# LayerNorm of all channels in token halves, with the last channel block's first-half convolution inside its own products

## The chip, the cores and the metric

One core of a Trainium2 chip runs the whole program. The metric is device time in microseconds (us) from the start of the program to its end; lower is better. The time given for a kernel is the median of its runs.

## The reference

One encoder layer on 512 tokens of 2048 channels, in float32: an RMSNorm; a pointwise product to 4096 channels, gated (`a * sigmoid(gate)`); a depthwise convolution of width 31 along the tokens; a LayerNorm over the channels of each token with gain and bias; `silu`; a second pointwise product (2048 to 2048), added to the input; then an RMSNorm, a squared-ReLU MLP of 8192 channels, another residual addition and a last RMSNorm. The change touches the end of the convolution, the LayerNorm and the beginning of the second pointwise product:

```python
u = lax.conv_general_dilated(u, w_dw[:, None, :], window_strides=(1,), padding=[(15, 15)], ...) + b_dw
u = jax.nn.silu(layer_norm(u, ln_g, ln_b))
return u @ w_pw2 + b_pw2
```

## The kernel before, in words

Channels lie on the 128 partitions and tokens along the free axis, so 2048 channels are 16 blocks of [128, 512]. Every float32 operand of a large product is split into a high part (ScalarE, ACT) and a low part (VectorE, DVE), and each product is three matmuls (`mm3`, L199): high by high, high by low, low by high. A weight piece is split by `split_hi` (L155, ACT) and `split_lo` (L164, DVE or POOL).

**First product and convolution.** `pw1` (L335) makes the two banks of one channel block j: 16 input blocks by 2 outputs by 3 matmuls. `glu` (L373) gates them into a padded buffer `u`. `conv_parts` (L390) returns the convolution of a block as three shares of the 31 taps: `on_pool` (ACT multiplies, POOL adds), `on_vector` (one multiply-add on DVE for each tap) and, for the last block alone, taps on TensorE (PE) by `conv_pe` (L452), whose stationary operands are 31-tap diagonals `dgw` (built at L520). The convolution of block j-1 runs beside the products of block j.

**The last block** (15) has no later products to run beside. Its products come in two token parts: `banks_a` (tokens 0 to 271, L526) and `banks_b` (L534). All work after them stands in one hand-written block (L619 to L705), inside which DVE, ACT and POOL keep the written order; PE keeps the written order throughout. It takes the first token half: 7 taps on POOL, 17 on DVE, 7 on PE; then the second half: 9, 14 and 8. `ln_sums` and `ln_last` (L543, L548) sum the channels by one-column matmuls into the bank `cols`; `ln_m2` to `ln_power` make variance and its power -1/2; `ln_mean` and `ln_scale` (L559, L584) spread mean and scale over the partitions by a matmul against a diagonal.

**LayerNorm of one block** is a chain of five instructions: `ln_a` (POOL adds the mean), `ln_b` (DVE multiplies by the scale; ACT applies Silu; ACT casts the high part), `ln_c` (DVE subtracts to get the low part). Blocks 0 to 7 are done in token halves, first all of half 0, later half 1; blocks 8 to 15 in full width by `ln` (L608).

**Second product.** `group` (L742) makes four banks from 16 blocks. In the first group (`split=4`) the blocks 0 to 7 (pieces 0 to 3) are multiplied for token half 0, then for half 1, then the blocks 8 to 15 in full width. At the places `LN_AT` in it stand `second_sums`, `second_mean` and `second_scale` (L707 to L736): the statistics of half 1 and the rest of the LayerNorm.

Of the kernel before, what the change touches and what calls it, by code (L numbers as in the profile page):

```python
# [14 lines left out]
P = 128  # L15
# [18 lines left out]
POOL_TAPS = [5, 5, 6, 5] * 3 + [6, 5, 9]  # L34
LAST_POOL, LAST_PE = (7, 9), (7, 8)
PE_TAPS = max(LAST_PE)
# [3 lines left out]
SUM_AT, SCALE_AT = (0, 15), (1, 13)  # L40
PE_AT = (2, 4)
SPLIT_AT = (1, 4)
NEXT_AT = 7
TAIL = (20, 7, 4, 2, 3)
LN_AT = ((0, 2, 2), (0, 3, 0), (0, 3, 1))
UNIT = 256
# [5 lines left out]
def conformer_layer(ctx: ExitStack, tc: tile.TileContext, xT, vecs, wdw, w1, w2, wupb, wdn, outT):  # L52
# [337 lines left out]
    def conv_parts(j, npool, t0=0, n=T, npe=0):  # L390
# [23 lines left out]
        def on_vector(c):  # L414
            acc = chain[(c - npool) % 2]
            src = acc
            if c == npool and j >= SHIFT_FROM:
                src = box["kb"][:, t0 : t0 + n]
# [32 lines left out]

    def conv_pe(acce, t0, n, i0, i1, npe):  # L452

        u = ubuf[(NK - 1) % 3]
        for i in range(i0, i1):
            c = CW - 1 - i
# [3 lines left out]
                rhs=u[:, t0 + c : t0 + c + n],  # L460
                start=i == 0,
                stop=i == npe - 1,
# [70 lines left out]
    sums(last - 1)  # L533
    banks_b = pw1(last, HT, HT)  # L534
    S, Q = box["S"], box["Q"]
# [7 lines left out]
    def ln_sums(h):  # L543
        t0 = HT * h
        colsum(cols, 4 * h, [S, box[last - 1][0]], t0, 2, h == 0, False, 1)
        colsum(cols, 4 * h + 2, [Q, box[last - 1][1]], t0, 2, False, False)

    def ln_last(h):  # L548
        t0 = HT * h
        colsum(cols, 4 * h, [vlast], t0, 2, False, True, 1)  # L550
        colsum(cols, 4 * h + 2, [sqlast], t0, 2, False, True)

# [3 lines left out]
    def ln_diag_mean(h):  # L556
        st[h]["dm"] = diag(cols[:, 4 * h : 4 * h + 2], f"mu{h}", ph1)

    def ln_mean(h):  # L559

        b = rstd[:, 0:HT]
        spread(st[h]["dm"], b, h == 1)
        nc.scalar.copy(out=mus[:, halves[h]], in_=b)

    def ln_m2(h):
        st[h]["m2"] = ph1.tile([P, 2], F32, name=f"m2{h}", bufs=1)
        nc.scalar.activation(out=st[h]["m2"], in_=cols[:, 4 * h : 4 * h + 2], func=AF.Square)

    def ln_var(h):
        st[h]["var"] = ph1.tile([P, 2], F32, name=f"var{h}", bufs=1)  # L570
        nc.vector.tensor_sub(out=st[h]["var"], in0=cols[:, 4 * h + 2 : 4 * h + 4], in1=st[h]["m2"])

# [13 lines left out]


    tmp = {}

    def ln_a(k, h):  # L590
        t = ph1.tile([P, T], F32, tag=("pc", "tg")[k % 2], name=f"lt{k}_{h}", bufs=2 - k % 2)[:, 0:HT]
        nc.gpsimd.tensor_add(out=t, in0=vg[k // 4][:, k % 4, halves[h]], in1=mus[:, halves[h]])
        tmp["t", k, h] = t

    def ln_b(k, h):
        t = ph1.tile([P, T], F32, tag=("vt", "ta")[k % 2], name=f"lu{k}_{h}", bufs=2 - k % 2)[:, 0:HT]
        nc.vector.tensor_mul(out=t, in0=tmp["t", k, h], in1=scale_of[h])
# [9 lines left out]

    def ln(k):  # L608
        t = ph1.tile([P, T], F32, tag="pc", name=f"lt{k}")
        nc.gpsimd.tensor_add(out=t, in0=vg[k // 4][:, k % 4], in1=mus)  # L610
        t2 = ph1.tile([P, T], F32, tag="vt", name=f"lu{k}")
        for h in range(2):
            nc.vector.tensor_mul(out=t2[:, halves[h]], in0=t[:, halves[h]], in1=scale_of[h])
        s = ph1.tile([P, T], F32, tag="pm", name=f"ls{k}", bufs=3)
        nc.scalar.activation(out=s, in_=t2, func=AF.Silu, scale=col(C_LNG, k), bias=col(C_LNB, k))
        nc.scalar.copy(out=sh[k], in_=s)
        nc.vector.tensor_sub(out=sl[k], in0=s, in1=sh[k].bitcast(F32))

    with tc.manual_schedule(engines=ordered):  # L619

        acc0, rstd = bank("mm", "acce0"), bank("x", "acce1")
        npool, npe = LAST_POOL[0], LAST_PE[0]
        on_pool, on_vector, join, vt, pc = conv_parts(last, npool, 0, HT, npe)
        npool1, npe1 = LAST_POOL[1], LAST_PE[1]
        on_pool1, on_vector1, join1, vt1, pc1 = conv_parts(last, npool1, HT, HT, npe1)
# [6 lines left out]

        for c in range(npool):
            on_pool(c)
            if c in SPLIT_AT:
                split_hi(n_p1 + 1 + SPLIT_AT.index(c))
        for c in range(npool, TAIL[0]):
            on_vector(c)
        conv_pe(acc0, 0, HT, 0, npe, npe)
        glu(last, *(b[:, EDGE - HT : HT] for b in banks_b), EDGE)  # L640
        some(1)
        cols = bank("y", "cols")
        scale_of = cols[:, HT:T], rstd[:, HT:T]
        ln_sums(0)
        conv_pe(rstd, HT, HT, 0, PE_AT[0], npe1)
        for c in range(TAIL[0], CW - npe - 2):
            on_vector(c)
        v = vlast[:, halves[0]]
        nc.vector.tensor_add(out=v, in0=pc[-1], in1=acc0[:, halves[0]])
        for c in range(CW - npe - 2, CW - npe):  # L650
            on_vector(c)
        join()
        nc.vector.tensor_add(out=v, in0=v, in1=vt)

        for c in range(5):
            on_pool1(c)
            if c == 2:
                split_hi(n_p1 + 3)
        ln_square(0)
        for c in range(5, TAIL[1]):  # L660
            on_pool1(c)
        some(TAIL[2])
        ln_last(0)
        conv_pe(rstd, HT, HT, PE_AT[0], PE_AT[1], npe1)
        ln_m2(0)
        ln_diag_mean(0)
        ln_var(0)
        ln_guard(0)
        ln_power(0)
        some(3)  # L670
        ln_mean(0)

        nc.scalar.activation(out=tiny, in_=ones[:, 0:1], func=AF.Silu)
        ln_diag_scale(0)
        ln_scale(0)
        conv_pe(rstd, HT, HT, PE_AT[1], npe1, npe1)
        ln_a(0, 0)
        ln_a(1, 0)
        for c in range(TAIL[1], npool1):
            on_pool1(c)  # L680
        some(TAIL[3])
        for k in range(0, 8, 2):
            if k < 6:
                ln_a(k + 2, 0)
                ln_a(k + 3, 0)
            ln_b(k, 0)
            ln_b(k + 1, 0)
            if k == 0:
                ln_sums(1)
            if k == 2:  # L690
                v = vlast[:, halves[1]]
                nc.vector.tensor_add(out=v, in0=pc1[-1], in1=rstd[:, halves[1]])
                some(99)
                ln_c(k, 0)
                join1()
                nc.vector.tensor_add(out=v, in0=v, in1=vt1)
                ln_square(1)
                ln_c(k + 1, 0)
            else:
                some(TAIL[4])  # L700
                ln_c(k, 0)
                ln_c(k + 1, 0)
            if k < 4:
                split_lo(n_p1 + 1 + k // 2, nc.vector)
        split_lo(n_p1 + 3, nc.gpsimd)  # L705

    def second_sums():  # L707
        ln_last(1)
        with tc.manual_schedule(engines=ordered):
# [3 lines left out]
            ln_guard(1)  # L713
            ln_power(1)
            ln_diag_scale(1)

    def second_mean():
        ln_mean(1)

    def second_scale():  # L720
        ln_scale(1)
        with tc.manual_schedule(engines=ordered):
            ln_a(0, 1)
            for k in range(8):
                if k < 7:
                    ln_a(k + 1, 1)
                ln_b(k, 1)
                if k:
                    ln_c(k - 1, 1)
                if k == NEXT_AT:  # L730
                    split_hi(n_p1 + 4)
                    split_lo(n_p1 + 4, nc.gpsimd)
            ln_c(7, 1)
        for k in range(8, NK):
            ln(k)
        p1.close()  # L736
# [72 lines left out]
    for g in range(4):  # L809
# [249 lines left out]
```

## Time and profile before

| | |
|---|---|
| median of 3 runs | 1942.65 us (1941.12 to 1948.48) |
| the profiled execution, its own time | 1946.38 us |
| its span, first to last instruction | 1944.6 us |
| PE busy in the span | 1913.9 us (98%) |
| first half of block 15's last products to the end of the first group of the second product | 347.2 to 436.4 us |

The profile shows one execution. A row of the timeline gives start, duration, engine, line, operation, and in brackets the idle time before it with what ended it; "x14" means 14 records merged. A float32 matmul of a tap, a sum or a spread has two records. [...]

### The profile page before, as it was taken

The page shows a single profiled execution, that of the slowest core. Times are in us where ns is not written, and L with a number is a line of the kernel's source. Part 1 is how long each engine was busy: PE and PEld are TensorE (multiplying, and loading weights), DVE is VectorE, ACT ScalarE, POOL GpSimd, SP SyncE. Part 2 cuts the span into 40 slices and gives each one's busy share as a digit, 9 for nine tenths or more (in the row PEclk, how much of TensorE's full clock was granted, in tenths as well). Part 3 has the DMA queues.
Part 4 walks back from the last instruction along what each step waited for, and adds up shares of the span by engine and source line. Part 5 has one row for each costly group of instructions (what it writes and reads, how often), then busy time and mean ns, then how long its engine had stood idle before and what let it go on. Part 6 is the DMA issues. An engine that isn't in the chain of part 4 may idle for free.

```text
span 1944.6 us, 27603 instructions
## 1 busy us (share of the span) xinstructions
PE 1913.9 (98%) x11192; PEld 1702.6 (88%) x11192; DVE 1389.9 (71%) x1911; ACT 741.1 (38%) x907; POOL 356.7 (18%) x243
## 2 busy tenths in 40 slices
PE   9999999899999999999999999999999999999997
PEld 7888888888879898998989899898989989899987
DVE  6999999875467675766767576676757667576844
ACT  6544444554344232423324233332423324242443
POOL 1789998741120000000000000000000000000000
PEclk9999999999999999999999999999999999999999
DMA  7332333143322333333233232323323233332332
GB/s 245 98 98 87 98 98 110 43 141 96 98 78 79 117 101 91 113 87 110 86 108 109 88 119 79 118 87 103 115 87 109 87 119 93 92 116 89 109 98 99
DMA packets 134558, 199.23 MB, mean 102 GB/s; under 512 B 7200, under 2 KB 72992, under 8 KB 134432
## 3 DMA queue, kind: packets, MB, share of 16 engines
q1 hardware_dynamic: 134288, 197.41, 33.1%
q8 instruction: 87, 1.43, 0.3%
q14 instruction: 39, 0.32, 0.1%
q10 hardware_dynamic: 144, 0.07, 0.0%
HBM read 193.27 MB, written 4.19 MB: 102 GB/s over the span
## 4 chain that ended last, share of the span: by engine, by line
issue 70%; PE 25%; DVE 4%; ACT 1%; POOL 1%; DMA 0%; SPq 0%; POOLq 0%; DVEq 0%; ACTq 0%
PE g L201 3%; PE g L202 3%; PE g L200 3%; PE pa L202 2%; PE pa L201 2%; PE pa L200 2%; PE pg L202 2%; PE pg L201 2%; PE pg L200 2%; DVE acc L426 2%; PE pa L363 1%; PE pg L363 1%; DVE slot L604 0%; POOL Q L841 0%; DMA wr<-w 0%
## 5 line engine op out<-in xcount | busy, mean ns | idle before, releaser
L162 ACT CAST wh<-wr 128x1024 fp32r<-128x1024 f32 x215 | 226.0, 1051 | 451.0 <-PE g L201 315.3
L200 PE MATMUL g<-z,wh 128*128 128x512 f32 (+1 forms) x1016 | 390.6, 384 | 0.0
L201 PE MATMUL g<-z,wh 128*128 128x512 f32 (+1 forms) x1016 | 390.3, 384 | 0.0
L202 PE MATMUL g<-z,wl 128*128 128x512 f32 (+1 forms) x1016 | 390.1, 384 | 0.0
L167 DVE TENSOR_TENSOR wl<-wr,wh 128x1024 fp32r<-128x1024 f32 x157 | 197.1, 1256 | 214.4 <-ACT wh L162 214.2
L202 PE MATMUL u<-slot,wl 128*128 128x256 f32 x1120 | 320.1, 286 | 3.6 <-DVE wl L186 2.6
L200 PE MATMUL u<-slot,wh 128*128 128x256 f32 x1120 | 318.1, 284 | 0.0
L201 PE MATMUL u<-slot,wh 128*128 128x256 f32 x1120 | 317.9, 284 | 0.0
L186 DVE TENSOR_TENSOR wl<-ws,wh 128x1024 fp32r<-128x1024 f32 x128 | 156.9, 1225 | 188.0 <-ACT wh L185 187.0
L248 POOL TENSOR_TENSOR rr_fin<-ms_fin,mhalf 128x2 f32<-128x2 f32 x2 | 1.4, 697 | 1341.5 <-DVE ms_fin L246 1341.5
L185 ACT CAST wh<-ws 128x1024 fp32r<-128x1024 f32 x128 | 134.4, 1050 | 289.9 <-DVE ws L183 135.1
L426 DVE SCALAR_TENSOR_TENSOR acc<-u,wd,acc 128x512 f32<-128x512 f32 (+1 forms) x362 | 239.0, 730 | 3.2 <-ACT acc L422 2.5
L202 PEld LDWEIGHTS g<-z,wl 128*128 128x128 f32 x1016 | 190.9, 188 | 37.8
L200 PEld LDWEIGHTS g<-z,wh 128*128 128x128 f32 x1016 | 191.0, 188 | 37.5
L201 PEld LDWEIGHTS g<-z,wh 128*128 128x128 f32 x1016 | 191.0, 188 | 37.1
L202 PEld LDWEIGHTS u<-slot,wl 128*128 128x128 f32 x1120 | 216.1, 193 | 7.4 <-DVE wl L186 6.6
L200 PEld LDWEIGHTS u<-slot,wh 128*128 128x128 f32 x1120 | 216.2, 193 | 0.0
L201 PEld LDWEIGHTS u<-slot,wh 128*128 128x128 f32 x1120 | 216.1, 193 | 0.0
L202 PE MATMUL u<-T,wl 128*128 128x256 f32 x672 | 190.6, 284 | 1.6 <-DVE wl L186 1.5
L200 PE MATMUL u<-T,wh 128*128 128x256 f32 x672 | 190.7, 284 | 1.0 <-ACT wh L185 1.0
L201 PE MATMUL u<-T,wh 128*128 128x256 f32 x672 | 190.1, 283 | 0.0
L178 ACT CAST wh<-wr 128x768 fp32r<-128x768 f32 x128 | 106.9, 835 | 214.5 <-PE g L201 123.0
(199 smaller groups left out, 3448.8 us busy)
## 6 DMA issues: line engine op xcount, KB each, us to landing
wr<-wupb SPq DMA_DIRECT2D x128, 512.0 KB, 3.6
wr<-wdn SPq DMA_DIRECT2D x128, 512.0 KB, 3.7
wr<-w SPq DMA_DIRECT2D x128, 256.0 KB, 3.2
wr<-w SPq DMA_DIRECT2D x32, 512.0 KB, 3.6
h<-xT SPq DMA_DIRECT2D x4, 1024.0 KB, 11.3
outT<-h SPq DMA_DIRECT2D x14, 256.0 KB, 2.8
x<-xT SPq DMA_DIRECT2D x6, 512.0 KB, 8.1
x<-xT SPq DMA_DIRECT2D x4, 256.0 KB, 4.9
```

Of the source, the lines that this page charges most:

```text
L162: nc.scalar.copy(out=prepped[i][0], in_=r)
L167: eng.tensor_tensor(out=lo, in0=r, in1=hi.bitcast(F32), op=ALU.subtract)
L178: nc.scalar.copy(out=hr, in_=r[:, :, 1:4])
L185: nc.scalar.copy(out=hs, in_=s)
L186: nc.vector.tensor_tensor(out=ls, in0=s, in1=hs.bitcast(F32), op=ALU.subtract)
L200: nc.tensor.matmul(out, lhsT=wh, rhs=xh, start=start, stop=False, **kw)
L201: nc.tensor.matmul(out, lhsT=wh, rhs=xl, start=False, stop=False, **kw)
L202: nc.tensor.matmul(out, lhsT=wl, rhs=xh, start=False, stop=stop, **kw)
L248: nc.gpsimd.tensor_tensor(out=r, in0=ms, in1=mhalf[:, 0:n], op=ALU.pow)
L363: nc.tensor.matmul(banks[j][s], lhsT=w[:, s, k % 2, c], rhs=x, start=k == 0 and x is ah[k] and w is wh, stop=stop)
L426: nc.vector.scalar_tensor_tensor(out=acc if c < end - 1 else vt, in0=u[:, c : c + n], scalar=wd[:, j, c : c + 1], in1=src, op0=ALU.mult, o ...
```

## The change

- The first token half of block 15 takes 7 taps on POOL, 8 on DVE and 16 on PE (before 7, 17 and 7); the second half 9, 12 and 10 (before 9, 14 and 8). `dgw` holds 16 diagonals, not 8.
- The first half's taps stand inside the products of `banks_b` before input block 8, and its sums, variance and power before input block 13 (`LAST_AT`).
- The LayerNorm is done in 32 units of one block and one token half, all 16 blocks of half 0 first, then all 16 of half 1 (`ln_to`). The full-width `ln` is gone.
- The first group splits at 5 pieces: blocks 0 to 9 in token halves, 10 to 15 in full width. The places `LN_AT` move.
- Both `split_lo` that ran on POOL here run on DVE. The shift `kb` has a copy `kbs` in SBUF for the second half.

```diff
-LAST_POOL, LAST_PE = (7, 9), (7, 8)
+LAST_POOL, LAST_PE = (7, 9), (16, 10)
+LAST_AT = (8, 13)
+SPLIT = 5
-LN_AT = ((0, 2, 2), (0, 3, 0), (0, 3, 1))
+LN_AT = ((0, 2, 0), (0, 3, 0), (0, 3, 2))
...
+    units = [(k, h) for h in range(2) for k in range(NK)]
...
     def ln_a(k, h):
-        t = ph1.tile([P, T], F32, tag=("pc", "tg")[k % 2], name=f"lt{k}_{h}", bufs=2 - k % 2)[:, 0:HT]
+        tag = ("tg", "ta", "lt")[(16 * h + k) % 3]
+        t = ph1.tile([P, HT if tag == "lt" else T], F32, tag=tag, name=f"lt{k}_{h}", bufs=1)[:, 0:HT]
...
+    def ln_to(n, ahead):
+
+        while done["c"] < n:
+            while done["a"] < min(done["b"] + 3, ahead):
+                ln_a(*units[done["a"]])
+                done["a"] += 1
+            if done["b"] < n:
+                ln_b(*units[done["b"]])
+                done["b"] += 1
+            if done["c"] < done["b"] - 1 or done["b"] == n:
+                ln_c(*units[done["c"]])
+                done["c"] += 1
...
+    def first_taps():
+        with tc.manual_schedule(engines=ordered):
+            for c in range(npool):
+                on_pool(c)
+                if c in SPLIT_AT:
+                    split_hi(n_p1 + 1 + SPLIT_AT.index(c))
+            for c in range(npool, CW - npe):
+                on_vector(c)
+            conv_pe(acc0, 0, HT, npe, True)
+
+    def first_sums():
+        box["cols"] = bank("y", "cols")
+        with tc.manual_schedule(engines=ordered):
+            join()
...
+            ln_square(0)
+            ln_sums(0)
+            ln_last(0)
+            ln_m2(0)
+            ln_diag_mean(0)
+            ln_var(0)
+            ln_guard(0)
+            ln_power(0)
+            split_lo(n_p1 + 1, nc.vector)
+            ln_diag_scale(0)
+
+    banks_b = pw1(last, HT, HT, hooks=dict(zip(LAST_AT, (first_taps, first_sums))))
...
+        glu(last, *(b[:, EDGE - HT : HT] for b in banks_b), EDGE)
+
+        nc.scalar.activation(out=tiny, in_=ones[:, 0:1], func=AF.Silu)
+        ln_mean(0)
+        ln_scale(0)
...
+        conv_pe(rstd, HT, HT, npe1, False)
+        split_lo(n_p1 + 2, nc.vector)
+        some(3)
+        for c in range(4):
             on_pool1(c)
...
+        split_hi(n_p1 + 3)
+        for n in range(1, 5):
+            ln_to(n, NK)
+            for c in range(4 + 2 * (n - 1), min(4 + 2 * n, npool1)):
+                on_pool1(c)
+            some(3)
+        ln_to(6, NK)
+        v = vlast[:, halves[1]]
+        nc.vector.tensor_add(out=v, in0=pc1[-1], in1=rstd[:, halves[1]])
+        some(99)
+        join1()
+        nc.vector.tensor_add(out=v, in0=v, in1=vt1)
+        ln_square(1)
+        ln_sums(1)
+        ln_to(8, NK)
+        split_lo(n_p1 + 3, nc.vector)
 
     def second_sums():
         ln_last(1)
...
             ln_power(1)
+            split_hi(n_p1 + 4)
+            ln_to(10, NK)
             ln_diag_scale(1)
+            split_lo(n_p1 + 4, nc.vector)
+            ln_to(12, NK)
 
     def second_mean():
-        ln_mean(1)
+        with tc.manual_schedule(engines=ordered):
+            ln_mean(1)
+            ln_to(14, NK + 1)
 
     def second_scale():
         ln_scale(1)
         with tc.manual_schedule(engines=ordered):
...
+            ln_to(2 * NK, 2 * NK)
         p1.close()
...
-        banks = group(NK, sh, sl, hooks, split=4 if g == 0 else 0)
+        banks = group(NK, sh, sl, hooks, split=SPLIT if g == 0 else 0)
```

## Rows read from the trace of the kernel before

**Rows 1.** The page's part 1: busy us (share of the span) xinstructions by engine.

```profile
PE 1913.9 (98%) x11192; PEld 1702.6 (88%) x11192; DVE 1389.9 (71%) x1911; ACT 741.1 (38%) x907; POOL 356.7 (18%) x243
```

**Rows 2.** Windows: length; busy us of PE, PEld, DVE, ACT, POOL; granted clock; DMA; GB/s.

```profile
347.20:358.70 11.50, 11.50 (x98) 11.50 (x97) 11.33 (x22) 7.40 (x12) 9.55 (x9) 1.00 0.01 2
358.70:375.80 17.10, 15.47 (x76) 12.96 (x74) 14.66 (x39) 10.69 (x23) 12.28 (x18) 0.80 0.00 0
375.80:436.40 60.60, 53.70 (x303) 47.58 (x303) 44.56 (x72) 31.98 (x56) 28.36 (x24) 0.92 0.41 137
...
386.20:393.60 7.40, 7.34 (x34) 7.23 (x35) 2.76 (x10) 1.98 (x5) 0.71 (x1) 0.54 0.25 71
...
412.90:417.00 4.10, 4.08 (x12) 3.22 (x13) 4.10 (x7) 1.43 (x2) 3.33 (x2) 0.62 0.57 167
```

**Rows 3.** PE's waits, 340 to 440 us: total us, times, longest us.

```profile
PE g L201 <- DVE slot L604: 3.7, 5, 2.3
PE g L201 <- DVE slot L617: 3.0, 1, 3.0
```

**Rows 4.** PE's timeline, from the last products' end to the first group's end.

```profile
358.73 3.18 PE L457 MATMUL acce<-u,dgw 128*128 128x256 f32 x14
363.54 0.58 PE L234 MATMUL cols<-invd,S 128*128 128x1 f32 x4 [1.63 <-DVE acc L426]
...
365.31 1.27 PE L457 MATMUL acce<-u,dgw 128*128 128x256 f32 x4
...
417.84 0.39 PE L200 MATMUL g<-slot,wh 128*128 128x512 f32 x1
...
434.16 0.39 PE L200 MATMUL g<-slot,wh 128*128 128x512 f32 x1
```

**Rows 5.** ACT's timeline: the diagonals early in the program, then the LayerNorm.

```profile
27.17 2.45 ACT L520 ACTIVATE dgw<-ident,wd 128x128 f32<-128x128 f32 x8
...
370.92 0.37 ACT L563 COPY mus<-acce 128x256 f32<-128x256 f32 x1 [2.60 <-PE acce L223]
371.31 1.28 ACT L673 ACT_TABLE_LOAD   x1
...
372.71 0.89 ACT L409 ACTIVATE pm<-u,wd 128x256 f32<-128x256 f32 x2
...
382.50 0.60 ACT L599 ACTIVATE ls<-lu,vec 128x256 f32<-128x256 f32 x1 [1.39 <-DVE lu L597]
383.13 0.41 ACT L600 CAST slot<-ls 128x256 fp32r<-128x256 f32 x1
```

**Rows 6.** DVE's timeline: taps, gate, LayerNorm, a weight split, the first group's output.

```profile
357.13 4.40 DVE L426 SCALAR_TENSOR_TENSOR acc<-u,wd,acc 128x256 f32<-128x256 f32 x11
...
362.39 0.47 DVE L381 SCALAR_TENSOR_TENSOR u<-ta,vec,tg 128x240 f32<-128x240 f32 x1 [0.25 <-ACT tg L378]
...
382.05 0.74 DVE L597 TENSOR_TENSOR lu<-lt,cols 128x256 f32<-128x256 f32 x2
...
390.43 0.42 DVE L213 TENSOR_TENSOR dg_mu<-ident,cols 128x256 f32<-128x256 f32 x1 [2.03 <-ACT m L567]
...
390.83 0.42 DVE L604 TENSOR_TENSOR slot<-ls,slot 128x256 fp32r<-128x256 f32 x1
...
394.96 0.42 DVE L597 TENSOR_TENSOR lu<-lt,acce 128x256 f32<-128x256 f32 x1 [2.38 <-POOL lt L592]
...
401.87 0.41 DVE L597 TENSOR_TENSOR lu<-lt,acce 128x256 f32<-128x256 f32 x1
...
413.45 1.21 DVE L167 TENSOR_TENSOR wl<-wr,wh 128x1024 fp32r<-128x1024 f32 x1
...
434.36 2.79 DVE L827 SCALAR_TENSOR_TENSOR h<-g,vec,h 128x512 f32<-128x512 f32 x4 [1.31 <-PE g L202]
```

**Rows 7.** POOL's timeline: the first half's last five tap additions.

```profile
358.28 3.96 POOL L411 TENSOR_TENSOR pc<-pc,pm 128x256 f32<-128x256 f32 x5
```

**Rows 8.** The low-part subtraction of line 604: ns min/median/max.

```profile
L604 DVE TENSOR_TENSOR slot<-ls,slot x16: 411/576/2628, 374.6 to 406.1; 128x256 fp32r<-128x256 f32 x16
```

More of the change, by code (lines that the diff above doesn't have):

```diff
@@ L417, in on_vector @@
             if c == npool and j >= SHIFT_FROM:
-                src = box["kb"][:, t0 : t0 + n]
+                src = box["kbs"] if t0 else box["kb"][:, 0:n]
             elif c < npool + 2:
@@ L450, in conv, with conv_pe @@
         nc.gpsimd.tensor_add(out=vg[j // 4][:, j % 4], in0=vt, in1=pc[-1])
-    def conv_pe(acce, t0, n, i0, i1, npe):
+    def conv_pe(acce, t0, n, npe, start):
         u = ubuf[(NK - 1) % 3]
-        for i in range(i0, i1):
+        for i in range(npe):
             c = CW - 1 - i
@@ L460, in conv_pe @@
                 rhs=u[:, t0 + c : t0 + c + n],
-                start=i == 0,
+                start=start and i == 0,
                 stop=i == npe - 1,
@@ L470, in shift @@
         nc.tensor.matmul(box["kb"], lhsT=nmean, rhs=vg[0][:, 0, :], start=True, stop=True)
+        box["kbs"] = ph1.tile([P, HT], F32, name="kbs", bufs=1)
+        nc.scalar.copy(out=box["kbs"], in_=box["kb"][:, HT:T])
     def sums(j):
@@ L533, in conformer_layer @@
     sums(last - 1)
-    banks_b = pw1(last, HT, HT)
     S, Q = box["S"], box["Q"]
@@ L544, in ln_sums @@
         t0 = HT * h
-        colsum(cols, 4 * h, [S, box[last - 1][0]], t0, 2, h == 0, False, 1)
-        colsum(cols, 4 * h + 2, [Q, box[last - 1][1]], t0, 2, False, False)
+        colsum(box["cols"], 4 * h, [S, box[last - 1][0]], t0, 2, h == 0, False, 1)
+        colsum(box["cols"], 4 * h + 2, [Q, box[last - 1][1]], t0, 2, False, False)
     def ln_last(h):
         t0 = HT * h
-        colsum(cols, 4 * h, [vlast], t0, 2, False, True, 1)
-        colsum(cols, 4 * h + 2, [sqlast], t0, 2, False, True)
+        colsum(box["cols"], 4 * h, [vlast], t0, 2, False, True, 1)
+        colsum(box["cols"], 4 * h + 2, [sqlast], t0, 2, False, True)
     def ln_square(h):
@@ L556, in ln_diag_mean @@
     def ln_diag_mean(h):
-        st[h]["dm"] = diag(cols[:, 4 * h : 4 * h + 2], f"mu{h}", ph1)
+        st[h]["dm"] = diag(box["cols"][:, 4 * h : 4 * h + 2], f"mu{h}", ph1)
     def ln_mean(h):
         b = rstd[:, 0:HT]
-        spread(st[h]["dm"], b, h == 1)
+        spread(st[h]["dm"], b)
         nc.scalar.copy(out=mus[:, halves[h]], in_=b)
@@ L566, in ln_m2 @@
         st[h]["m2"] = ph1.tile([P, 2], F32, name=f"m2{h}", bufs=1)
-        nc.scalar.activation(out=st[h]["m2"], in_=cols[:, 4 * h : 4 * h + 2], func=AF.Square)
+        nc.scalar.activation(out=st[h]["m2"], in_=box["cols"][:, 4 * h : 4 * h + 2], func=AF.Square)
     def ln_var(h):
         st[h]["var"] = ph1.tile([P, 2], F32, name=f"var{h}", bufs=1)
-        nc.vector.tensor_sub(out=st[h]["var"], in0=cols[:, 4 * h + 2 : 4 * h + 4], in1=st[h]["m2"])
+        nc.vector.tensor_sub(out=st[h]["var"], in0=box["cols"][:, 4 * h + 2 : 4 * h + 4], in1=st[h]["m2"])
     def ln_guard(h):
@@ L585, in ln_scale @@
         spread(st[h]["dr"], scale_of[h], h == 1)
+    units = [(k, h) for h in range(2) for k in range(NK)]
+    done = {"a": 0, "b": 0, "c": 0}
     tmp = {}
     def ln_a(k, h):
[L591 removed]
+        tag = ("tg", "ta", "lt")[(16 * h + k) % 3]
+        t = ph1.tile([P, HT if tag == "lt" else T], F32, tag=tag, name=f"lt{k}_{h}", bufs=1)[:, 0:HT]
         nc.gpsimd.tensor_add(out=t, in0=vg[k // 4][:, k % 4, halves[h]], in1=mus[:, halves[h]])
@@ L606, in ln_c @@
         )
[L608 to L617, printed above, removed]
+    def ln_to(n, ahead):
[9 more added lines that the diff above has]
+                done["c"] += 1
@@ new lines, in conformer_layer @@
+    npool, npe = LAST_POOL[0], LAST_PE[0]
+    npool1, npe1 = LAST_POOL[1], LAST_PE[1]
+    acc0 = bank("mm", "acce0")
+    on_pool, on_vector, join, vt, pc = conv_parts(last, npool, 0, HT, npe)
+    def first_taps():
[7 more added lines that the diff above has]
+            conv_pe(acc0, 0, HT, npe, True)
@@ new lines, in first_sums @@
+    def first_sums():
+        box["cols"] = bank("y", "cols")
+        with tc.manual_schedule(engines=ordered):
+            join()
+            v = vlast[:, halves[0]]
+            nc.vector.tensor_add(out=v, in0=pc[-1], in1=acc0[:, halves[0]])
+            nc.vector.tensor_add(out=v, in0=v, in1=vt)
+            ln_square(0)
[8 more added lines that the diff above has]
+            ln_diag_scale(0)
@@ L619, in conformer_layer @@
+    banks_b = pw1(last, HT, HT, hooks=dict(zip(LAST_AT, (first_taps, first_sums))))
+    cols, rstd = box["cols"], bank("x", "acce1")
+    scale_of = cols[:, HT:T], rstd[:, HT:T]
     with tc.manual_schedule(engines=ordered):
[L621 to L624, printed above, removed]
+        glu(last, *(b[:, EDGE - HT : HT] for b in banks_b), EDGE)
+        nc.scalar.activation(out=tiny, in_=ones[:, 0:1], func=AF.Silu)
+        ln_mean(0)
+        ln_scale(0)
@@ L631, in some @@
                     on_vector1(taps.pop(0))
[L633 to L655, printed above, removed]
-            on_pool1(c)
[L657 to L704, printed above, removed]
@@ L722, in second_scale @@
         with tc.manual_schedule(engines=ordered):
[L723 to L735, printed above, removed]
+            ln_to(2 * NK, 2 * NK)
         p1.close()
```

6 lines of the change are left out of this document (1 added, 5 removed).

## The prediction

> **What bounds the kernel now.** I read the page's engine line first: PE is busy 98% of the span [rows 1], so time can only come from stretches where PE stalls, or runs at the lower clock. Next the windows of the stretch that the change touches. The last products (347.2 to 358.7) are dense at a granted clock of 1.00. The 17.1 us behind them are 15.47 busy at 0.80, and the first group of the second product takes 60.6 us with 53.7 busy at 0.92 [rows 2]. Undisturbed, that group would need 192 half-width matmuls at 11.5 / 96 = 0.12 us [rows 2] and 96 full-width ones at 0.227 us (434.16 less 417.84 is 72 of them) [rows 4], 44.8 us; sums and spreads add some 2.5. So about 13 us are lost in the group, and a few ahead of it: under 20 us, 1% of the time, is all that there is to win. What loses it is in PE's waits: 3.7 us for the low parts of line 604, once 2.3 in one piece, and 3.0 for one of line 617 [rows 3], both from DVE. After each of the two long ones the granted clock is lower: 0.54 for 7.4 us and 0.62 for 4.1 us [rows 2], which costs 0.46 x 7.4 + 0.38 x 4.1 = 5 us more. So LayerNorm output, not PE, sets the pace there.
>
> **The change, part by part.** I follow the path to the point where PE can start token half 1 of the first group, since from there only PE work remains.
>
> *Taps and sums inside the products.* PE has 11.5 us of products [rows 2], then 16 taps where there were 7. Seven take 3.18 [rows 4], 0.45 each, so 7.3 us. The sums take 365.31 - 363.54 = 1.77 [rows 4]; the four last ones half that, 0.9. So banks_b is complete at 347.2 + 11.5 + 7.3 + 1.8 + 0.9 = 368.7. PE should not wait in it: POOL's part of the taps ends at 358.28 + 3.96 = 362.2 [rows 7], three additions and a square follow in about 1.5 us, and PE needs the result at about 367.8. The old 1.63 us wait of the sums [rows 4] goes: it hung on the second half's first tap reading `kb`, which now is a copy. DVE saves nine taps of 0.40 in the first half and two in the second [rows 6], but the first nine were beside the products and PE waits for POOL's part, so they shorten nothing there.
>
> *The gate of the second half.* `u` is complete at 362.39 + 0.47 = 362.9 now [rows 6]. After the change it follows 368.7 by about 1.9 (two products with the scale, sigmoid, one more): 370.6. PE then does ten taps, 4.5, and the second half's early sums, 1.8: 376.9. The group begins about 1 us later than the 375.8 of now, whatever DVE has won.
>
> *The first unit of the LayerNorm.* ACT's order behind the sigmoid (370.1) is table load 1.28, mean copy 0.37 [rows 5], then the tap products; POOL's order is three tap additions (3.96 / 5 = 0.79 each [rows 7]) ahead of the first `ln_a`. 370.1 + 1.8 + two products 0.89 [rows 5] + 2.4 + 0.79 = 376.0. The load moves from behind the mean copy to before it, so all of it lies on this path. [...]
>
> *Units 0 to 3.* One unit costs, from the DVE product to the end of the low part, 0.45 (382.05 to 382.50, [rows 5, 6]) + 0.63 (to 383.13) + 0.44 + 0.41 (the shortest subtraction [rows 8]) = 1.93. `ln_to(1)` to `ln_to(4)` finish one unit each before anything else: DVE stands while ACT works, and the nine taps written between (0.40 each) do not fill that hole, as they are queued behind the subtraction. 4 x 1.93 + 3.6 = 11.3: 387.3.
>
> *Units 4 to 13.* Written in pairs: 0.45, two ACT passes of 0.95 (0.63 + 0.31 of overlap), a subtraction, 2.9 a pair. In between come the second half's three additions (1.05), two `split_lo` of 1.21 [rows 6] (both moved here from POOL; they are not long, but each stands ahead of a pair), and the statistics on DVE, about 1.2 from the 0.42 of one diagonal [rows 6]. Five pairs 14.5 + 1.05 + 2.4 + 1.2 = 19.2: 406.5.
>
> *Units 14 to 16.* Unit 16 is half 1 of block 0. In the open stream a unit takes (401.87 - 394.96) / 6 = 1.15 [rows 6]. 1.93 + 2.3 = 4.2: 410.7. Now half 1 begins at about 394.96 + 1.93 = 397 [rows 6], because only 8 units stand ahead of it.
>
> *From there.* Half 1 of ten blocks, 120 matmuls of 0.12 = 14.4, and 72 full-width ones, 16.3 [rows 4]: 441.4. PE has done its ten blocks of half 0 at about 404 and then stands 5 to 6 us, so I add one stretch at the lower clock, about 2 us, as after the two long stalls now [rows 2]: 443.4. The order of parts is not rigid: now the main block's last subtraction runs at 390.83, behind the next part's diagonal at 390.43 [rows 6]. I take 1 us off: 442.4. The group ends now at 434.36 + 3 x 0.68 = 436.4 [rows 6]. The difference is **+6 us**.
>
> *At nothing.* Eight more diagonals are 2.45 us of ACT at 27 us [rows 5], where PE is paced by products and has input blocks in hand; without that cover, up to 2.5. The `kbs` copy is one ACT instruction on an idle engine. No DMA is issued anew or at another place in SP's order; the loads of `h` wait for the LayerNorm's inputs to be read, which ends near 425 and leaves them 15 us, and the group after this one does not need them. Two more blocks in halves cost PE 2 x (24 x 0.12 - 12 x 0.227) = 0.3, inside the sum. What I don't know is how far parts overlap and what POOL's additions do to DVE; these bound the sum by -5.5 and +8.
>
> The profiled run's own time is 1946.4 (span 1944.6), 3.7 us above the median of 1942.65 and inside its spread, so I put the difference on the median: **1948.5 us**. What a measurement can tell from no change is about 0.5%, 9.7 us: below 1932.9 is faster, above 1952.4 slower.
>
> **The rivals.**
>
> *The parts overlap fully.* If the pairs of `second_sums`, `second_mean` and `second_scale` fill each other's holes, units 8 to 16 run at ACT's 0.95, 8.6 us plus one weight split, and half 1 starts at 405: the sum is about +0.5 us, 1943. For it: the order of 390.43 and 390.83. Against: inside a part the order is written, and ACT's next part begins with the mean copy, which waits for PE.
>
> *POOL's additions hold up DVE.* The subtraction takes 0.41 at best but 0.58 at the median and 2.63 once [rows 8]. After the change POOL has 32 half-width additions and DVE 32 subtractions. If 17 of them and the three weight splits before half 1 each lose the gap of 0.2 to 0.4, that is 3.4 to 8 us more: 1952 to 1956, slower. Against: POOL's two weight splits, its longest instructions there, are gone, and in a pair its additions fall while DVE waits for ACT. [...]
>
> *DVE's relief counts and PE is the bound.* If DVE, ACT and POOL overlap well from the first unit (one unit in 0.95 to 1.0 from 376), unit 16 is ready at 393, when PE has finished half 0. Then the group runs from 376.9 without a stall, 45.2 + 2.5: 424.5, a gain of 12 us, 1931, faster. It decides if a unit costs under about 1.05 us on average over the first 17, taps included. Against: 12 taps, three splits and the one-at-a-time order of units 0 to 3, which alone take 11 us for four units.
>
> **How the numbers follow.** Forecast, PE waiting for unit 16 with the end between +2 and +9.7: 0.55. Overlap, -5 to +2: 0.20. POOL holds up DVE, above +9.7: 0.20. PE the bound, below -9.7: 0.05. So faster 0.05, same 0.75, slower 0.20. The range leaves out the fast rival and the far half of the slow one: 1939 to 1957.
>
> **What would show it.** Right: in the first group one long PE wait of 4 to 7 us for a low part at the start of token half 1, near 410, and shorter ones of 1 to 3 us between 377 and 387, one for each of units 1 to 3; no wait in the sums of the first half; the group's end near 442. Wrong: no long wait near 410, or token half 1 starting before 400; or subtractions at 0.8 us and more throughout, which is the slow rival; or PE waiting inside banks_b for the first half's value, which would mean that POOL's taps come later than now.

## The result, and the profile after

The changed kernel took 1961.03 us (median of 4 runs, 1959.51 to 1963.17) beside 1944.14 us of the kernel before (4 runs): a ratio of 1.0084 [1.0071, 1.0097]. The forecast of 1948.5 us had the sign, but 1961.03 lies outside its range of 1939 to 1957. The profiled execution took 1963.17 us, span 1961.4.

Cutting both spans at two points tells where the loss lies: at the first product of block 15's last stage, and at the first output instruction of the first group (before: DVE L827 at 434.36 [rows 6]; after: L812 at 446.75). The stretch between them, called the region below, takes 99.18 us before and 111.66 after: **+12.5**. The rest to the end of the span, the tail, takes 1510.24 before and 1514.65 after: **+4.4**, in code that the diff does not touch. Up to the region nothing moved (335.18 and 335.09).

The engine line of the page:

```profile
PE 1921.5 (98%) x11238; PEld 1711.7 (87%) x11238; DVE 1381.0 (70%) x1910; ACT 747.6 (38%) x932; POOL 353.4 (18%) x249
```

PE's busy time is 7.6 us more than in [rows 1], with 46 matmuls more. Eleven more taps on PE are 22 of them, about 5.0 us at 0.45 a tap [rows 4]; two more blocks in halves are the other 24, forecast at 0.3. The other 2.3 us lie in the tail, where the number of matmuls is the same. The windows (columns as in [rows 2]; the granted clock is TensorE's, as a share of its full speed):

```profile
358.70:369.70 11.00, 11.00 (x78) 10.86 (x77) 4.21 (x10) 1.64 (x5) 4.74 (x6) 0.84 0.05 4
...
378.90:391.90 13.00, 3.46 (x17) 3.42 (x17) 8.40 (x22) 6.44 (x15) 7.66 (x11) 0.67 0.01 1
391.90:399.90 8.00, 8.00 (x49) 8.00 (x50) 2.99 (x5) 2.16 (x5) 1.43 (x2) 0.69 0.22 67
...
414.20:448.80 34.60, 34.27 (x193) 30.76 (x194) 20.93 (x40) 20.47 (x38) 10.41 (x12) 0.90 0.57 196
```

The products of the last stage now run on without a wait to 369.7, as forecast, but not all at a granted clock of 1.00: behind the one-column sums (363.38 to 366.0, granted clock 1.00, PE never idle) the stretch from 366.0 to 369.7 was granted 0.54. The hole is the second line: 13 us in which PE is busy for 3.46. The third shows what it leaves behind, 8 us at 0.69. PE's waits between 340 and 448 us name it (total us, times, longest); of the two of [rows 3], 6.7 us together, 0.3 is left:

```profile
PE cols L234 <- DVE lu L600: 9.5, 1, 9.5
PE g L200 <- ACT slot L603: 3.8, 1, 3.8
PE acce L457 <- ACT mus L563: 1.9, 1, 1.9
PE g L201 <- DVE slot L607: 0.3, 1, 0.3
```

PE's timeline puts them in order:

```profile
363.38 0.50 PE L234 MATMUL cols<-invd,S 128*128 128x1 f32 x4
...
370.14 0.59 PE L223 MATMUL cols<-dg_lnr,ones 128*128 128x256 f32 x2
372.67 6.27 PE L457 MATMUL acce<-u,dgw 128*128 128x256 f32 x20 [1.94 <-ACT mus L563]
388.48 1.02 PE L234 MATMUL cols<-invd,S 128*128 128x1 f32 x4 [9.54 <-DVE lu L600]
...
391.92 0.56 PE L200 MATMUL g<-slot,wh 128*128 128x256 f32 x1
...
414.24 0.58 PE L200 MATMUL g<-slot,wh 128*128 128x256 f32 x1 [3.80 <-ACT slot L603]
```

The first half's sums (363.38) run without a wait. After its ten taps PE reaches the second half's early sums (L234, `S` and `Q` of the first 15 blocks, whose inputs have long been there) and stands for 9.54 us behind `lu`, the DVE product of the LayerNorm. The two share no data. They share the bank `cols`: columns 0 to 7 hold the channel sums, columns 256 to 511 the scale of half 0, written by the spread at 370.14, which each product `lu` of half 0 reads. In the program `ln_sums(1)` stands behind the products of the first six units, and in the trace PE writes into the bank only behind the read of the sixth (388.43, below). The first group is queued behind the sums on PE and starts at 391.92, not 376.9. In this kernel the sums and the scale are also two parts of one tile, and no run here separates the tile from the bank.

DVE's timeline shows both sides of this, and what it does further on:

```profile
376.71 0.42 DVE L600 TENSOR_TENSOR lu<-lt,cols 128x256 f32<-128x256 f32 x1 [3.05 <-POOL lt L595]
378.24 0.43 DVE L607 TENSOR_TENSOR slot<-ls,slot 128x256 fp32r<-128x256 f32 x1 [1.10 <-ACT slot L603]
378.58 1.27 DVE L426 SCALAR_TENSOR_TENSOR acc<-u,wd,acc 128x256 f32<-128x256 f32 x3
379.76 0.41 DVE L600 TENSOR_TENSOR lu<-lt,cols 128x256 f32<-128x256 f32 x1
...
387.69 0.74 DVE L600 TENSOR_TENSOR lu<-lt,cols 128x256 f32<-128x256 f32 x2
...
392.52 0.75 DVE L600 TENSOR_TENSOR lu<-lt,cols 128x256 f32<-128x256 f32 x2 [0.83 <-PE cols L234]
...
401.12 0.42 DVE L213 TENSOR_TENSOR dg_mu<-ident,cols 128x256 f32<-128x256 f32 x1 [4.57 <-ACT m L567]
...
446.75 2.79 DVE L812 SCALAR_TENSOR_TENSOR h<-g,vec,h 128x512 f32<-128x512 f32 x4 [1.32 <-PE g L202]
```

The units 4 and 5 read at 387.69 and end at 388.43; the sums start 0.05 us later, at 388.48. Units 6 and 7 then wait 0.83 for the sums: the bank goes back and forth. At 401.12 DVE has stood 4.57 us for the statistics of half 1, which come late because their sums (`ln_last(1)`) are queued on PE behind the late group, at 399.93; in e5 below, where the group is not late, this wait is 0.38. So the late start is handed on to unit 16, the first of half 1, and PE stands a second time at 414.24.

### The profile page after: what moved, and what is told of

The parts are those of the page before. It is cut to its first block, busy times and chain, and to the rows that moved or that the text cites. A ratio compares the mean times of both kernels' runs of the same rounds, so it can differ in the third digit from the quotient of the medians.

```text
span 1961.4 us, 27731 instructions
## 1 busy us (share of the span) xinstructions
PE 1921.5 (98%) x11238; PEld 1711.7 (87%) x11238; DVE 1381.0 (70%) x1910; ACT 747.6 (38%) x932; POOL 353.4 (18%) x249
## 4 chain that ended last, share of the span: by engine, by line
issue 69%; PE 28%; DVE 1%; ACT 1%; POOL 1%; DMA 0%; POOLq 0%; SPq 0%; DVEq 0%; ACTq 0%
PE g L201 3%; PE g L200 3%; PE g L202 3%; PE pa L201 3%; PE pa L200 3%; PE pg L201 3%; PE pg L200 3%; PE pa L202 3%; PE pg L202 3%; PE pa L363 1%; PE pg L363 1%; POOL Q L826 0%; PE cols L234 0%; PE acce L457 0%; ACT ls L602 0%
## 5 line engine op out<-in xcount | busy, mean ns | idle before, releaser
L186 DVE TENSOR_TENSOR wl<-ws,wh 128x1024 fp32r<-128x1024 f32 x128 | 156.8, 1225 | 188.6 <-ACT wh L185 187.9
L185 ACT CAST wh<-ws 128x1024 fp32r<-128x1024 f32 x128 | 134.1, 1048 | 287.3 <-DVE ws L183 131.0
L426 DVE SCALAR_TENSOR_TENSOR acc<-u,wd,acc 128x512 f32<-128x512 f32 (+1 forms) x351 | 234.4, 737 | 3.3 <-ACT acc L422 2.6
```

What stands on the lines that cost most here:

```text
L185: nc.scalar.copy(out=hs, in_=s)
L186: nc.vector.tensor_tensor(out=ls, in0=s, in1=hs.bitcast(F32), op=ALU.subtract)
L426: nc.vector.scalar_tensor_tensor(out=acc if c < end - 1 else vt, in0=u[:, c : c + n], scalar=wd[:, j, c : c + 1], in1=src, op0=ALU.mult, o ...
```

## The experiments

All regions and tails below are cut as above, from each kernel's profiled run.

| kernel | median us (runs) | ratio to before | region | tail |
|---|---|---|---|---|
| before | | | 99.18 | 1510.24 |
| after | 1961.03 (4) | 1.0084 [1.0071, 1.0097] | 111.66 | 1514.65 |
| e1_sums_early | 1960.14 (5) | 1.0074 [1.0061, 1.0087] | 108.00 | 1513.04 |
| e2_scale_sbuf | 1958.16 (6) | 1.0065 [1.0053, 1.0078] | 108.23 | 1513.73 |
| e3_before_late | 1954.43 (5) | 1.0044 [1.0032, 1.0056] | 103.53 | 1512.26 |
| e4_mlp_order | 1960.77 (6) | 1.0072 [1.0056, 1.0088] | 111.84 | 1511.51 |
| e5_chain_scale | 1954.66 (6) | 1.0049 [1.0036, 1.0063] | 105.59 | 1512.19 |
| e8_order_only | 1950.29 (8) | 1.0026 [1.0014, 1.0037] | 104.13 | 1509.63 |
| e6_chain_order | 1945.48 (12) | 1.0001 [0.9992, 1.0011] | 99.79 | 1509.17 |
| e7_best | 1936.46 (6) | 0.9957 [0.9943, 0.997] | 91.83 | 1508.20 |

The kernel before took 1945.31 us beside the first four experiments (11 runs) and 1945.14 beside the others (18 runs), so times are best compared by the ratios. What stands ahead of the region took 334.6 to 335.3 us in most of these profiled runs and 336.6 to 337.3 in three (e1, e2, e3).

In e6, e7 and e8 the cut itself moves. There the first output waits not for PE but for the load of `h`:

```profile
438.77 2.73 DVE L811 SCALAR_TENSOR_TENSOR h<-g,vec,h 128x512 f32<-128x512 f32 x4 [2.87 <-DMA h<-xT]
434.83 2.73 DVE L811 SCALAR_TENSOR_TENSOR h<-g,vec,h 128x512 f32<-128x512 f32 x4 [3.51 <-DMA h<-xT]
```

The first row is of e8, the second of e6; in e7 the profile names PE, but the row (426.80) stands only 0.19 us ahead of the start of PE's last matmul of the first group (426.99), where elsewhere it is 1.6, so the load is taken as the cause there too. PE has meanwhile gone on to the next group. Counted to the start of that last matmul, the stretch is 100.79 before, 113.27 after, 107.20 in e5, 104.10 in e8, 99.21 in e6 and 92.02 in e7. Below, this is called PE's stretch.

### Is it the place of the sums: e1_sums_early

```diff
         conv_pe(rstd, HT, HT, npe1, False)
+        ln_sums(1)
         split_lo(n_p1 + 2, nc.vector)
...
         ln_square(1)
-        ln_sums(1)
         ln_to(8, NK)
```

> The changed kernel, with the early sums of token half 1 moved to directly behind the ten taps on TensorE, ahead of every LayerNorm unit. Theory A (one PSUM bank, cols, holds these sums and the scale of half 0, so the sums wait for the DVE products of units 0 to 5 that read the scale): the PE wait of 9.5 us at the sums is gone, the first group begins near 378, token half 1 near 410 and not 414, the first output of the group (L812 there) near 441 and not 446.8; about 5 to 6 us off the changed kernel, near 1955. Theory B (the units on DVE and ACT set the pace, the wait hides behind them): token half 1 begins at 414 as before and the time stays within 1.5 us of 1961. What follows the first group's end (1514.7 us in the changed kernel, 1510.2 in the kernel before) stays 1514 to 1515 in both.

The wait of 9.54 us is gone, as expected, but the region is only 3.7 us shorter, and the time is 14.8 us above the kernel before, where it was 16.9. DVE's timeline has the first unit:

```profile
381.01 0.42 DVE L600 TENSOR_TENSOR lu<-lt,cols 128x256 f32<-128x256 f32 x1 [5.38 <-PE cols L234]
```

Counted from the region's start (337.26 in this run, 335.09 in the changed kernel's) the first product of the LayerNorm comes after 43.75 us, 2.1 later than in the changed kernel (376.71 - 335.09 = 41.62), because now it is the reader that waits for the writer of the same bank, and PE reaches the sums only behind ten taps. PE's waits show the rest (total us, times, longest):

```profile
PE g L200 <- ACT slot L603: 9.0, 5, 4.2
PE cols L234 <- DVE lu L600: 1.9, 1, 1.9
```

With one bank for both, the order of the program only chooses who waits: in the changed kernel the sums, 9.54 us, here the first product, 5.38 us. The expectation missed in size because it moved the wait's one end and did not ask who stands at the other.

### Is it the bank: e2_scale_sbuf

```diff
-        nc.vector.tensor_mul(out=t, in0=tmp["t", k, h], in1=scale_of[h])
+        nc.vector.tensor_mul(out=t, in0=tmp["t", k, h], in1=scale_of[1] if h else box["sc0"])
...
         ln_scale(0)
+        box["sc0"] = box["rmix"][:, 0:HT]
+        nc.scalar.copy(out=box["sc0"], in_=cols[:, HT:T])
```

> The changed kernel, with the scale of token half 0 copied by ACT from the bank cols to SBUF and read from there by the DVE products; the sums of half 1 stay where they are, behind unit 5. Theory A (the bank): the 9.5 us wait goes although the sums have not moved, PE passes them near 378, and the time falls by 4 to 6 us as with the sums moved, less what POOL's additions now do to a DVE product with two SBUF inputs (up to 0.3 us a unit). Rival (the place in the written order holds the sums back, through some other tie to units 0 to 5): the wait stays at 8 to 10 us and the time at 1961.

PE's timeline has the sums at their old place in the program, behind six products that now read SBUF, and without a wait:

```profile
380.33 0.50 PE L234 MATMUL cols<-invd,S 128*128 128x1 f32 x4
```

So it is the sharing of `cols` and nothing else about the sums. The region is only 3.4 us shorter, though; the copy has a price of its own. DVE's timeline of the first four products:

```profile
378.52 0.95 DVE L600 TENSOR_TENSOR lu<-lt,rmix 128x256 f32<-128x256 f32 x1 [3.31 <-POOL lt L595]
382.10 0.82 DVE L600 TENSOR_TENSOR lu<-lt,rmix 128x256 f32<-128x256 f32 x1
385.54 0.82 DVE L600 TENSOR_TENSOR lu<-lt,rmix 128x256 f32<-128x256 f32 x1
388.99 0.70 DVE L600 TENSOR_TENSOR lu<-lt,rmix 128x256 f32<-128x256 f32 x1
```

With the scale in PSUM each takes 0.41 to 0.42 (above). They now have two inputs in SBUF, and POOL's additions run beside all four: 0.3 to 0.5 us lost in each, 1.6 together. Two of these additions are longer as well, 0.90 and 0.93 us where the same two take 0.72 and 0.73 in the changed kernel. Two inputs in SBUF alone do not explain it, since most later products of half 0 lose nothing (0.41, or 0.75 for two); that it is POOL's additions beside them fits these rows, but no run here separates it.

### The bank without a new price: e5_chain_scale

Here the scale of half 0 is spread into the bank of the tap chain, which is idle by then: PSUM still, but not the bank of the sums.

```diff
-        spread(st[h]["dr"], scale_of[h], h == 1)
+        spread(st[h]["dr"], scale_of[h])
...
-    scale_of = cols[:, HT:T], rstd[:, HT:T]
+    scale_of = box["chain"][0][:, 0:HT], rstd[:, HT:T]
```

> The changed kernel, with the scale of token half 0 spread into the bank of a DVE tap chain, whose half-0 part is free by then, and no longer into cols. Nothing is reordered, and a DVE product still has one input in PSUM. Theory A (the shared bank alone): the sums pass without a wait, the first unit is not held up either, and from the start of the last block's products to the first output of the group (111.7 us in the changed kernel, 99.2 before, 108.0 with the sums moved) it is 105.5 to 107.5; PE's waits are then for the high parts of units 1 to 3, 1 to 2 us each, and 4 to 5 us at token half 1. Rival (the wait was worth no more than the 3.6 us that the sums moved gave): 108.

The region is 105.59: the shared bank costs **6.1 us** (111.66 - 105.59). PE's timeline has the shape that the prediction had drawn for the changed kernel:

```profile
378.31 0.50 PE L234 MATMUL cols<-invd,S 128*128 128x1 f32 x4
...
380.83 0.38 PE L200 MATMUL g<-slot,wh 128*128 128x256 f32 x1 [0.21 <-ACT slot L603]
...
384.07 0.38 PE L200 MATMUL g<-slot,wh 128*128 128x256 f32 x1 [0.16 <-ACT slot L603]
...
387.10 0.58 PE L200 MATMUL g<-slot,wh 128*128 128x256 f32 x1 [2.08 <-ACT slot L603]
...
408.16 0.58 PE L200 MATMUL g<-slot,wh 128*128 128x256 f32 x1 [3.57 <-ACT slot L603]
```

There are short waits between 380 and 387 for the units done one at a time, then one of 3.57 at the start of half 1, at 408.16. That the wait of 9.54 was worth only 6.1 is read here in part: without it PE stands 2.45 us in three pieces for the units themselves. Nor is the wait's length its price: in e4, which leaves this region as it is in the changed kernel, the same wait came out at 11.2 us in a region of 111.84. It is 11.2 in e8 too, behind ten taps of 4.59 us, where those of the changed kernel took 6.27 at a granted clock of 0.73.

### The same fault in the kernel before: e3_before_late

```diff
-            if k == 0:
+            if k == 4:
                 ln_sums(1)
```

> The kernel before, with the early sums of token half 1 moved from behind units 0 and 1 to behind units 4 and 5 of half 0. Theory A: PE waits 8 to 9 us at the sums for the DVE product of unit 5 and the first group begins near 384 instead of 375.8; part of that is hidden since PE waited for units 2 to 5 anyway, so the group's end is 3 to 5 us later. The compiled DVE order at the start of the MLP also comes out as in the changed kernel (the first output addition ahead of a weight piece's last subtraction), so if that order is what costs 4 us there, the rest behind the group is 1514 and not 1510, and the sum is 7 to 9 us over the kernel before. Rival (no bank tie, and 4 us later on are chance): the time stays within 2 us of the kernel before.

This is the kernel before with one place changed: the same sums stand behind the products of six units, not two. PE's timeline:

```profile
384.04 1.02 PE L234 MATMUL cols<-invd,S 128*128 128x1 f32 x4 [9.29 <-DVE lu L597]
```

The wait appears in a kernel that has nothing else of the change, and the region grows by 4.35 us. The time grows by 9.1; in the profiled runs the tail is 2.0 us longer (below), and 1.9 lie ahead of the region, where nothing was edited. Here the place of the sums behind six reads of their bank is enough for 9.29 us.

### The order of the units: e8_order_only and e6_chain_order

PE needs half 0 of ten blocks and then half 1 of ten; the changed kernel makes 16 units of half 0 first. Here ten and ten come first, then the other twelve; e8 keeps the scale in `cols`.

```diff
-    units = [(k, h) for h in range(2) for k in range(NK)]
+    NH = 2 * SPLIT
+    units = [(k, h) for h in range(2) for k in range(NH)] + [(k, h) for k in range(NH, NK) for h in range(2)]
...
-            ln_to(10, NK)
+            ln_to(10, NH)
             ln_diag_scale(1)
             split_lo(n_p1 + 4, nc.vector)
-            ln_to(12, NK)
...
-            ln_to(14, NK + 1)
```

> The changed kernel, with the units in the order in which TensorE consumes them: blocks 0 to 9 of half 0, blocks 0 to 9 of half 1, then 10 to 15, both halves. The shared bank stays. Theory D (16 units ahead of half 1 where 10 are consumed first): the 3.8 us wait at token half 1 is gone or under 1 us and the stretch falls from 111.7 to 106.5 to 108.5 us; the 9.5 us wait at the sums stays. The MLP's compiled order comes out as in the kernel before, so the rest is 1510 to 1512 and the whole near 1953. Rival (DVE, ACT and POOL are at their rate, whatever the order): a wait of the same size comes later, at blocks 10 to 15, and the stretch stays above 110.

PE's waits, of which the first stays (11.2 us, as in e4) and the one at half 1 is gone:

```profile
PE cols L234 <- DVE lu L601: 11.2, 1, 11.2
PE acce L457 <- ACT mus L563: 1.3, 1, 1.3
```

The region is 104.13: the order is worth **7.5 us** alone, more than expected, and 9.2 by PE's stretch. e6_chain_order has both edits, of e5 and of e8:

> Both of the last two: the scale in the chain's bank and the units in the order of use. Theories A and D together: the stretch is 99 to 102 us, about that of the kernel before, and the rest 1510 to 1512; the time is within 4 us of the kernel before. What is left as waits is one for each of units 1 to 3 (1 to 2 us each), since each of these is finished on DVE before the next begins. Rival: the two waits cover each other, and the pair gives no more than the better one alone (106 to 107).

The region is 99.79, 11.9 us less than in the changed kernel, where the two alone gave 6.1 and 7.5: they nearly add up (14.1 beside 6.1 and 9.2 by PE's stretch). That is about the region of the kernel before again (99.18), and the time is the same, 1.0001 [0.9992, 1.0011].

### The tail: e4_mlp_order

The tail grew by 4.4 us with no edit in it. The DVE order there is chosen by a scheduler, not written out, and it came out differently at the first unit of the MLP; what in the edits turns it is not known. DVE's timeline of the kernel before:

```profile
595.61 1.22 DVE L186 TENSOR_TENSOR wl<-ws,wh 128x1024 fp32r<-128x1024 f32 x1 [1.19 <-ACT wh L185]
597.03 0.69 DVE L892 TENSOR_TENSOR c<-u,q 128x512 f32<-128x512 f32 x1 [0.19 <-PE sp_ffn L223]
```

And of the changed one, where L877 is the same output addition as L892:

```profile
607.20 0.43 DVE L183 TENSOR_TENSOR ws<-ws,wr 128x256 f32<-128x256 f32 x1
610.53 0.69 DVE L877 TENSOR_TENSOR c<-u,q 128x512 f32<-128x512 f32 x1 [2.91 <-PE sp_ffn L223]
611.14 1.21 DVE L186 TENSOR_TENSOR wl<-ws,wh 128x1024 fp32r<-128x1024 f32 x1
```

The addition stands ahead of the weight piece's last subtraction, DVE waits 2.91 us in it for the spread, and the weights come late to PE:

```profile
618.96 0.38 PE L200 MATMUL u<-T,wh 128*128 128x256 f32 x1 [1.35 <-ACT wh L185]
620.22 0.38 PE L202 MATMUL u<-T,wl 128*128 128x256 f32 x1 [0.76 <-DVE wl L186]
```

e4 puts the old order back:

```diff
-        nc.vector.tensor_tensor(out=c[:, 2:6:2], in0=two(banks[1]), in1=bc(q1), op=ALU.add)
+        if u == 0:
+            with tc.issue_after(getattr(state["ls"], "ins", state["ls"])):
+                nc.vector.tensor_tensor(out=c[:, 2:6:2], in0=two(banks[1]), in1=bc(q1), op=ALU.add)
...
```

> The changed kernel, with one order edge more: in the first MLP unit the first output addition on DVE is issued behind the last subtraction of the weight piece prepared before it, as in the kernel before. Nothing else is touched. Theory C (the compiled DVE order there, which the change shifted without naming it, costs 4 us): the DVE wait of 2.9 us for the spread of the scale and the PE waits of 1.4 and 0.8 us behind it go, what follows the first group is 1510 to 1511.5 instead of 1514.7, and the time falls by 3 to 4 us to about 1957.5. Rival (the 4 us are the phase of the clock behind the 3.2 us wait for the sum of squares, chance of a run): within 1 us of 1961.

In the profiled run PE's waits for `wh` of L185 between 560 and 700 us are 0.5 us in all where they were 1.9, those for `wl` of L186 2.8 where they were 3.3, and the tail is 3.1 us shorter, 1511.51. The times do not show it: 15.5 us above the kernel before where the changed kernel was 16.9, with overlapping intervals, in runs that spread over 6.6 us (1955.69 to 1962.31). Alone it settles nothing. The ten profiled runs together speak for it: five kernels with the new order (after, e1, e2, e3, e5) have tails of 1512.19 to 1514.65, mean 1513.2; the five with the old one (before, e4, e6, e7, e8) 1508.20 to 1511.51, mean 1509.8. They do not overlap and lie 3.4 us apart. Three of the old-order tails are short partly because their cut waits for `h`; counted from PE's last matmul of the first group the means are 1511.6 and 1509.2, 2.4 apart, and the nearest two 0.7. So 2.4 to 3.4 of the 4.4 us go with the order in the profiles; that they are the cause is likely, not shown.

### Both edits and a looser written order: e7_best

To e6's two edits it adds a looser written order: weight splits move into the time when DVE and ACT stood for the first half's sums, the load of the Silu table moves behind the mean copy and three tap products, each product of the LayerNorm is written ahead of the low part before it, with taps between. The early sums of half 1 stand directly behind the ten taps, and the first place of `LN_AT` moves from (0, 2, 0) to (0, 2, 2). The cut shows a part of it:

```diff
             ln_square(0)
+            split_lo(n_p1 + 1, nc.vector)
+            split_lo(n_p1 + 2, nc.vector)
+            split_hi(n_p1 + 3)
             ln_sums(0)
...
-        nc.scalar.activation(out=tiny, in_=ones[:, 0:1], func=AF.Silu)
         ln_mean(0)
...
+        on_pool1(2)
+        nc.scalar.activation(out=tiny, in_=ones[:, 0:1], func=AF.Silu)
...
+        lnb()
+        some(3)
+        on_pool1(3)
+        lna()
+        lnb()
+        lnc()
...
```

> The pair before, with the hand-written order of the last part loosened: weight splits moved into DVE's and ACT's idle time during the first half's sums, the Silu table loaded after the first tap products of half 1, and each unit's low part written behind the next unit's product, with taps between. Theory: the holes of units 0 to 3 (1.1 us each) close, PE waits under 3 us in all between the taps and block 10, and the stretch is 90 to 95 us, 4 to 9 us under the kernel before; time 1936 to 1941 where the kernel before gives 1945. Rival (ACT and POOL are the pace of units 0 to 7, at some 1.8 us a unit with the taps): 96 to 99, no gain over the kernel before.

It took 1936.46 us, 0.9957 [0.9943, 0.997] of the kernel before. PE's waits in the region, all that the view lists:

```profile
PE g L201 <- DVE slot L608: 1.8, 3, 1.0
PE g L202 <- DVE wl L167: 0.7, 1, 0.7
```

And its timeline at the taps, which in the changed kernel waited 1.94 us for the mean copy on ACT, itself behind the table load:

```profile
370.81 4.56 PE L457 MATMUL acce<-u,dgw 128*128 128x256 f32 x20
375.21 0.50 PE L234 MATMUL cols<-invd,S 128*128 128x1 f32 x4
...
380.89 0.38 PE L201 MATMUL g<-slot,wh 128*128 128x256 f32 x1 [0.42 <-DVE slot L608]
```

The region is 91.83, 8.0 us below e6's (7.2 by PE's stretch). Which of the edits gave how much of it was not measured.

## Why the prediction was right or wrong

**The forecast's sum was right for a kernel without the bank wait.** It put the region's growth at 6; e5 shows 6.4 (105.59 - 99.18). The loss splits as 6.4 (forecast 6) + 6.1 (the bank) in the region and 4.4 in the tail, 16.9 in all.

**Points that held.** Taps and sums inside the products, without a wait: banks_b was to be done at 368.7 and is at 369.7, the stretch of the 18 products behind the sums (366.0 to 369.7) having been granted 0.54. `u` complete: 370.6, measured 371.35. First unit: 376.0, measured 376.71. Units 0 to 3: 11.3 us for four, measured 11.0 from the first product to that of unit 4 (376.71 to 387.69), three units of 3.04 with taps between and one of 1.86 without. The table load on the path, 1.28 us as in [rows 5]; ACT's timeline after:

```profile
370.35 0.49 ACT L378 ACTIVATE tg<-tg,vec 128x240 f32<-128x240 f32 x1 [4.03 <-DVE tg L377]
370.86 1.28 ACT L663 ACT_TABLE_LOAD   x1
...
372.26 0.35 ACT L563 COPY mus<-acce 128x256 f32<-128x256 f32 x1
```

The load starts 0.02 us behind the sigmoid, and the mean copy starts 0.12 us behind the load's end. Half 1 and the rest, counted from the region's start: the forecast has half 1 after 74.5 us (410.7 less the 1 us of overlap, less 335.18) and then 30.7 to the first output (32.7 to the group's end less three outputs of 0.68). In e5, whose region starts at 334.62, half 1 begins after 73.5 and 32.1 follow. So the LayerNorm was 1.0 better and PE's remainder 1.4 worse; until 413.55 its half-width matmuls followed one another 0.21 us apart or more. Part of this is luck: in e5 units 4 to 13 took 15.5 us where 19.2, less the 1 for overlap, was forecast, the first unit came 0.8 later and units 14 to 16 took 1.0 more. The load of `h` was forecast to have time to spare; it had in the changed kernel, and set the first output in e6 and e8.

**The step that failed** is "PE then does ten taps, 4.5, and the second half's early sums, 1.8: 376.9. The group begins about 1 us later". The sums waited 9.54 us behind `lu`, the reader of their bank, and the group began at 391.92. With the scale in another bank the wait is gone and the region 6.1 us shorter (e5). The sums were costed as work of PE whose inputs are ready, which they are; what they write into was not looked at. The evidence was in hand: the prediction explains the old wait of 1.63 us of the same sums [rows 4] by a DVE tap that read another tile of that bank, and takes it as gone because that tap now reads a copy. That the scale of half 0 lies in the same bank, and that the change writes the sums behind six of its readers where before it was two, stands in the code. The smaller wait of the taps has the same form (1.94 us; the bank `acce1` is read by the mean copy) and was not forecast either: 372.67 is where the prediction has the taps begin at 370.6. The taps themselves were costed at 4.5 us and took 6.27 at a granted clock of 0.73. So even in e5 the group begins 3.7 us later than forecast, counted from the region's start (380.01 - 334.62 = 45.4, against 376.9 - 335.18 = 41.7); it does not show in the sum, since unit 16 decides when half 1 begins.

**A second step** is "At nothing": the prediction allowed nothing outside the stretch. Code whose order a scheduler picks came out in another order 160 us later, and the tail lost 4.4 us, of which 2.4 to 3.4 go with that order by ten traces; the cause of the whole stays open.

**The rivals.** The outcome was the slow one, by another mechanism than the rival's. POOL's additions did little to DVE: the low-part subtraction took 0.43 at the median against the 0.58 of [rows 8], and what the first 17 took beyond 0.41 each adds up to about 2 us, where the rival had 3.4 to 8. One row of the whole LayerNorm after, ns min/median/max:

```profile
L607 DVE TENSOR_TENSOR slot<-ls,slot x32: 408/426/973, 378.2 to 434.5; 128x256 fp32r<-128x256 f32 x32
```

The prediction's signs came out in part: the long wait near 410 came at 414.24, with 3.80 us just under the 4 to 7 and for a high part, not a low one; the short ones between 377 and 387 came only in e5 and smaller (0.21, 0.16, 2.08); and what stood in their place was named nowhere, not among the signs of being wrong either. The fast rival, PE as the bound, had the right reasons against it (the one-at-a-time order of units 0 to 3); e7, which loosens that order, takes the region 7.4 us below the kernel before.

## What to carry to other kernels

When a write of PE is moved, list who reads its bank (or tile: no run here separates the two), any column of it, and which of these readers the new place puts ahead of it: here the sums waited 9.54 us for the last of them (9.29 in e3), and the group queued behind them on PE waited too. If two uses of a bank must interleave, give one of them another bank; a copy to SBUF can eat a good part of what it frees (here 3.4 us were left of 6.1). Order the units of a producer by when the consumer takes them, not by what is convenient to loop over, and after an edit compare the order of code that a scheduler arranges, also where nothing was edited.

## What the runs showed of the hardware that was not expected

The first four DVE products of 128x256 with both inputs in SBUF took 0.70 to 0.95 us beside POOL's additions (e2), and 0.41 to 0.42 beside them with one input in PSUM, in the same place of the program (the changed kernel). PE was slower behind the wait of 9.54 us as well: the sums ran at a granted clock of 0.50 (388.48 to 391.92) and the first 8.0 us of the group at 0.69; until 396.8 its half-width matmuls followed one another 0.21 us apart, and 0.12 from there on. What that cost here was not measured; the last sums of half 1, for which DVE stood, are queued behind it. And the clock fell without a wait too: after 2.6 us of one-column sums, with PE busy throughout, the products from 366.0 to 369.7 were granted 0.54, which is estimated at 0.46 x 3.7 = 1.7 us. In e5 and e8 their distance goes from 0.12 to 0.21 us in the same stretch, 0.5 and 1.2 us behind the sums.
